# A norm factor by one matmul and a wide power on GpSimd, a last product in column halves, and more fill work before a recurrence's last level

## The chip, the cores and the metric

The kernel runs on one core of a Trainium2 chip. The core has five engines that run side by side and wait for each other through semaphores: TensorE (PE in the profile, with its weight loads as PEld), VectorE (DVE), ScalarE (ACT), GpSimd (POOL) and SyncE (SP, which here only issues DMAs). Matrix products land in PSUM, which DVE and ACT read; everything else lies in SBUF. The metric is device time in microseconds (us) of one execution, lower is better; a time before or after is the median of several executions.

## The reference

One layer of a streaming encoder on 512 tokens of width 1024, batch 1, all in float32. Cut to what matters here:

```python
def rmsnorm(x, g):
    y = x * lax.rsqrt(jnp.mean(x * x, axis=-1, keepdims=True) + EPS)
    return y * g

hn = rmsnorm(h, norm_mix_g[l])
proj = hn @ w_in[l]
fox_out = fox_attention(...)          # 8 heads of 64, causal
rec = hgrn2_chunkwise(...)            # 4 heads, state 128x128, gated recurrence
h = h + jnp.concatenate([fox_out, rec], axis=-1) @ w_out[l]
h = h + memory_cross_attention(rmsnorm(h, norm_x_g[l]), mem_n, w_xq[l], w_xkv[l], w_xo[l])
u = rmsnorm(h, norm_ff_g[l]) @ w1[l]
h = h + jnp.square(jax.nn.relu(u)) @ w2[l]
return rmsnorm(h, final_norm_g)
```

Three places bear on the change: the mean square in the norm ahead of the MLP (`rmsnorm(h, norm_ff_g)`), the MLP's second product (`@ w2`) with the last norm behind it, and the gated recurrence (`hgrn2_chunkwise`).

## The kernel before

Nearly every product is done three times in a reduced float format (hi*hi, lo*hi, hi*lo of operands that ACT and DVE split into a high and a low part), so a product of a 128-wide block of 1024 inputs is 24 matmuls of 128x512. The order on PE is written out by hand; a scheduler sets the order on the other engines from its own estimates.

**The recurrence** (loop over `mlev`, levels m = 1 to 64). At each level ACT builds two `mix` tiles for each of two pairs of heads (L682, L683), PE multiplies them (`lv`, L689), and DVE and POOL update the factors. While these run, PE takes pieces of other projections from a queue `fill`: `fill.run(us)` issues queued matmuls for about so many microseconds, here `2 * F2` = 5.4 behind each level. Ahead of the last level (`li == 6`), `gate_rows` transposes a small tile on PE (`pFr`, L661). The queue holds the projection `gg` there, of which ACT evicts each finished token tile (L588).

**The norm ahead of the MLP.** The residual is held transposed (channels on partitions, the 512 tokens along the free axis). `ssq2` [128x512] sums the squares over the eight channel blocks on POOL (L1038, L1039). `mean_sq` (L1048) sums it over the partitions by four fp32 matmuls with a column of ones, whose result has tokens on partitions ([128x4], `pm`); DVE divides by D, POOL adds EPS (L360, tile `r2e`) and raises it to -1/2 (L363, a `tensor_tensor` with `op=pow` and a tile `mhalf` of -0.5). Four more fp32 matmuls (L1405) spread the four columns over all partitions with the tokens along the free axis again, and DVE copies that to `rbc2` [128x512] (in the profile `rbc`, the tile it shares).

**The MLP.** Hidden blocks are made in eight groups of 512 channels, each four tiles `u` in PSUM (24 matmuls each, L234 to L236). The tiles lie in the pool `mm`, which has three buffers. `square` empties one: DVE multiplies relu(u) by `rbc2` (L1269, tile `ur`), ACT squares it (L1272). So no `u` is emptied before `rbc2` is there, and the fourth `u` tile needs the first one's buffer. In the code `mean_sq` stands between the first and the second `u` tile, the spreading matmuls between the second and the third.

**The second product** is done by a scheme of seven products on quarters (`PRODUCTS`, with `PLAN` for the PSUM bank and where each goes); weight combinations are made by DMAs that add, issued from POOL (L1207). In the last call of `mlp_down` the last product "4" lands in bank `U` behind "1", "6" and "7", for token tile 2 first and tile 3 second; the bank is added to `acc` by DVE (L1299), and `finish` does the last norm of that tile: DVE sum of squares (L1365), POOL power -1/2 (L1367, [128x1]), then ACT (L1369) and DVE (L1371) each scale one half of the columns and two DMAs store them.

Of the kernel before, what the change touches and what calls it, by code (L numbers as in the profile page):

```python
# [12 lines left out]
AF = mybir.ActivationFunctionType  # L13
ALU = mybir.AluOpType
# [19 lines left out]
P1, P2, P3, P4, PW = 20, 20, 20, 10, -20  # L34
MT, NF, V0, LAG = 3, 2, 1, 3
F1, F2, F3, F4, B1 = 1.6, 2.7, 1.5, 1.0, 2.0
A1, A2 = 1.4, 0.8
X1, X2, X3, X4 = 1.5, 2.0, 1.5, 2.0
NEG = -3.0e38
# [3 lines left out]
def emit(  # L43
# [78 lines left out]
    def tr(name, shape=(S,)):  # L122
        return trp.tile([P] + list(shape), F32, tag="tr", name=name)
# [233 lines left out]
    def rstd_of(ms, n, name, r=None):  # L357

        e = sm(n, name + "e")
        gp.tensor_scalar(e, ms, 1.0, EPS, op0=ALU.mult, op1=ALU.add)  # L360
        if r is None:
            r = sm(n, name)
        gp.tensor_tensor(r, e, mhalf[:, 0:n], op=ALU.pow)  # L363
        return r
# [304 lines left out]
    for li, m in enumerate(mlev):  # L669
        if li == 3:  # L670
            fill.until("ff")
            gates()
        if li == 5:
            gate_sums()
        if li == 6:
            gate_rows()
        lvs = []
        for hp in range(2):
            M_ = Mv[hp]
            mix = t2(f"mix{hp}{m}", F32, (NT, P))  # L680
            mv_ = halves(mix.rearrange("p c t -> p (c t)"), m)
            ac.activation(mv_[:, :, 0, :], halves(kt_(2 * hp), m)[:, :, 0, :], AF.Copy)  # L682
            ac.activation(mv_[:, :, 1, :], halves(qt_(2 * hp + 1), m)[:, :, 1, :], AF.Copy)  # L683
            w = 64 if m == 64 else 32
            ps = sc(f"lv{hp}{m}", (NT, 2, w))
            for c in range(NT):
                for o in range(0, P, 2 * w):
                    rhs = bass.AP(M_.tensor, M_.offset + c * P + o + m, [list(M_.ap[0]), [S - m, 2], [2 * m, w // m], [1, m]])
                    te.matmul(ps[o : o + 2 * w, c].rearrange("p u (b m) -> p u b m", m=m), mix[:, c, o : o + 2 * w], rhs, start=True, stop=True)  # L689
            lvs.append(ps)  # L690
        for hp, ps in enumerate(lvs):
            F_ = Fg[hp]
            if m < 64:
                for j in range(2):
                    ve.copy_predicated(
                        Ac[hp][:, 4 * j : 4 * j + 4].rearrange("p c (b two m) -> p c b two m", two=2, m=m)[:, :, :, 1 - j, :],
                        mku[:, j, li, :].rearrange("p (b m) -> p b m", m=m).unsqueeze(1).to_broadcast([P, NT, w // m, m]),
                        ps[:, :, j, :].rearrange("p c (b m) -> p c b m", m=m),
                    )
            else:  # L700
                A_ = s4([8, P], f"A{hp}")
                Ag.append(A_)
                lo_, hi_ = slice(0, 64), slice(64, P)
                gp.memset(A_[hi_, 0:4, lo_], 0.0)
                gp.memset(A_[lo_, 4:8, hi_], 0.0)
                for r in (lo_, hi_):
                    ac.activation(A_[r, :, r], Ac[hp][r], AF.Copy)
                ve.tensor_copy(A_[lo_, 0:4, hi_], ps[lo_, :, 0, :])
                ve.tensor_copy(A_[hi_, 4:8, lo_], ps[hi_, :, 1, :])
            for j in range(2):  # L710
                h = 2 * hp + j
                qv, kv, fv = halves(qt_(h), m), halves(kt_(h), m), halves(F_[:, j, :], m)
                bshape = [P, S // (2 * m), m]
                ve.tensor_tensor(qv[:, :, 1, :], qv[:, :, 1, :], fv[:, :, 0, 0:1].to_broadcast(bshape), ALU.mult)
                (ve, gp)[j].tensor_tensor(kv[:, :, 0, :], kv[:, :, 0, :], fv[:, :, 1, 0:1].to_broadcast(bshape), op=ALU.mult)
            fv = halves(F_.rearrange("p h t -> p (h t)"), m)
            gp.tensor_tensor(fv[:, :, 0, 0:1], fv[:, :, 0, 0:1], fv[:, :, 1, 0:1], op=ALU.mult)
        fill.run(2 * F2)
    fq, fk = {}, {}

    def fox_proj(p):
# [323 lines left out]
    def mean_sq(ssq, name):  # L1045
        pm = tr(name, (NT,))
        for tb in range(NT):
            te.matmul(pm[:, tb : tb + 1], ssq[:, tb * P : (tb + 1) * P], ones, start=True, stop=True)  # L1048
        ms = sm(NT, name + "m")
        ve.tensor_scalar(ms, pm, 1.0 / D, None, op0=ALU.mult)  # L1050
        return ms
# [262 lines left out]
    def mlp_down(gs):  # L1314

        end = gs[-1] == NG - 1
        banks = {}
        for n, name in enumerate(PRODUCTS):
            bank, first_, goes = PLAN[name]

            both = [(g, t) for g in gs for t in range(2)]
            for g, t in both if name != PRODUCTS[-1] else sorted(both, key=lambda gt: gt[1]):
                whi, wlo = unit("d", g, name)
                hb = hbs[g, name]
                if first_ and g == gs[0]:
                    banks[bank, t] = {"U": sc, "Y": tr, "V": mm}[bank](f"{bank}{g}{t}")
                ps = banks[bank, t]
                ts_ = slice(t * P, (t + 1) * P)
                for k in range(2):
                    hi, lo = hb[:, 0, k, ts_], hb[:, 1, k, ts_]  # L1330
                    begin = first_ and g == gs[0] and k == 0
                    te.matmul(ps, hi, whi[:, k, :], start=begin, stop=False, skip_group_check=True)  # L1332
                    te.matmul(ps, hi, wlo[:, k, :], start=False, stop=False, skip_group_check=True)  # L1333
                    te.matmul(ps, lo, whi[:, k, :], start=False, stop=k == 1, skip_group_check=True)  # L1334
                if end and (g, t) == (gs[0], 1) and 1 <= n < len(PRODUCTS) - 1:
                    hidden_part(NG - 1, PRODUCTS[n + 1])
                for rows, half, sign in goes if g == gs[-1] else ():
                    add_to(ps, rows, half, t, sign)
                    if end and (name, rows) in FINAL:
                        finish(2 * rows + t, half)  # L1340
            if not end:
                hidden_part(gs[0] + 1, name)
            elif n == 0:
                hidden_part(NG - 1, PRODUCTS[1])
# [5 lines left out]
    def finish(tb, half):  # L1350

        a = acc[tb]
        cs = slice(half * S, (half + 1) * S)
        if tb not in fin:
            e = sm(1, f"fe{tb}")
            ac.activation(t2(f"fj{tb}"), a[:, cs], AF.Square, scale=1.0 / 32.0, accum_out=e)
            gp.tensor_scalar(e, e, 1.0, EPS, op0=ALU.mult, op1=ALU.add)
            ag = t2(f"fa{tb}")
            gp.tensor_tensor(ag, a[:, cs], gfin[half], op=ALU.mult)
            fin[tb] = (e, cs, ag)  # L1360
            return
        e, cs0, ag = fin[tb]
        o = s4([D], f"fo{tb}")
        v = sm(1, f"fv{tb}")
        ve.tensor_tensor_reduce(out=o[:, cs], in0=a[:, cs], in1=a[:, cs], scale=1.0 / D, scalar=e, op0=ALU.mult, op1=ALU.add, accum_out=v)  # L1365
        r = sm(1, f"fr{tb}")
        gp.tensor_tensor(r, v, mhalf[:, 0:1], op=ALU.pow)  # L1367
        rows = slice(tb * P, (tb + 1) * P)
        ac.activation(o[:, cs0], ag, AF.Identity, scale=r)  # L1369
        ac.dma_start(out[rows, cs0], o[:, cs0])  # L1370
        ve.scalar_tensor_tensor(o[:, cs], a[:, cs], r, gfin[half], op0=ALU.mult, op1=ALU.mult)  # L1371
        nc.sync.dma_start(out[rows, cs], o[:, cs])

    def mlp_up_group(g):
        for j in range(2):
            if g < 2:
                wt = next_panel()
                if (g, j) == (0, 0):
                    down_raws(0)
                elif (g, j) == (1, 1):  # L1380
                    for _ in range(2):
                        unit_q.popleft()[1]()
            else:
                wt = tuple(list(x) for x in zip(*(unit("u", g, j, n) for n in range(2))))
                if (g, j) == (NG - 1, 0):
                    load_raws(g, RAWS[0:3])
            yield from mlp_up(g, j, wt)
# [9 lines left out]
    rbc2 = rbc  # L1397
    ups = mlp_up_group(0)
    up0 = next(ups)
    ms2 = mean_sq(ssq2, "pm2")  # L1400
    r2 = rstd_of(ms2, NT, "r2")
    up1 = next(ups)
    pb = tr("rbc2")
    for tb in range(NT):
        te.matmul(pb[:, tb * P : (tb + 1) * P], r2[:, tb : tb + 1].to_broadcast([P, P]), ident, start=True, stop=True)  # L1405
    ve.tensor_copy(rbc2, pb)
    square(*up0)
    square(*up1)
    for up in ups:
# [42 lines left out]
```

## Time and profile before

| what | value |
|---|---|
| median of 3 executions | 778.06 us (776.39 to 778.52) |
| the profiled execution | 778.45 us |
| its span, first to last instruction | 776.7 us |
| mean granted TensorE clock | 0.996 |
| instructions | 11208 |
| DVE, ACT, POOL busy | 525.6, 367.0, 193.9 us |
| DMA moved | 103.03 MB, mean 133 GB/s |

The time outside the span is 778.45 - 776.7 = 1.75 us. In the profile's rows a group has its line, engine, operation, output and inputs, shape and count, then busy time and mean duration, then the idle time of that engine just before and who ended it. A row of the timeline has start, duration, engine, line, operation and tiles, in microseconds from the span's start.

### The profile page before, as it was taken

What the parts mean: (1) busy time and instruction counts of PE and PEld (TensorE: products, weight loads), DVE (VectorE), ACT (ScalarE), POOL (GpSimd) and SP (SyncE); (2) the same over time, 40 slices, a digit from 0 to 9 for tenths busy, and PEclk for the clock granted to TensorE, in tenths of its full rate; (3) what the DMA queues carried; (4) which work ended last, traced back from release to release, by engine and by line L of the source; (5) the groups of instructions that cost most, each with busy time, mean ns of one, the idle gap of its engine ahead of it and who ended that gap; (6) DMA issues with size and microseconds to landing.
All of it is one profiled execution on the core that took longest, in us unless ns stands there. A gap on an engine that the chain in (4) does not pass through costs nothing.

```text
span 776.7 us, 11208 instructions
## 1 busy us (share of the span) xinstructions
PE 763.2 (98%) x4212; PEld 644.8 (83%) x4212; DVE 525.6 (68%) x846; ACT 367.0 (47%) x616; POOL 193.9 (25%) x262
## 2 busy tenths in 40 slices
PE   7999999999999999999999999999999999999995
PEld 5889988988979988888888888888888888888884
DVE  3746864687577656645538646959686768777795
ACT  4664555675565532344434344535353435352552
POOL 7106532424343015410006520100101010101123
PEclk9999999999999999999999999999999999999998
DMA  6642421142443442312212596575848475758602
GB/s 203 215 127 77 143 83 55 55 130 71 161 136 131 135 156 89 108 57 81 81 54 82 180 281 136 154 172 163 189 136 207 131 181 160 190 136 229 123 1 108
DMA packets 79831, 103.03 MB, mean 133 GB/s; under 512 B 4593, under 2 KB 58394, under 8 KB 79778
## 3 DMA queue, kind: packets, MB, share of 16 engines
q1 hardware_dynamic: 70226, 76.61, 31.3%
q0 software_dynamic: 8960, 24.67, 14.9%
q10 hardware_dynamic: 592, 1.05, 0.4%
q8 instruction: 33, 0.54, 0.3%
q14 instruction: 20, 0.16, 0.1%
HBM read 89.71 MB, written 4.21 MB: 121 GB/s over the span
## 4 chain that ended last, share of the span: by engine, by line
PE 97%; DMA 1%; DVE 1%; issue 0%; POOL 0%; SPq 0%; POOLq 0%; ACT 0%; DVEq 0%; ACTq 0%
PE u L235 7%; PE u L234 7%; PE u L236 7%; PE U L1333 4%; PE U L1334 4%; PE U L1332 3%; PE xq L234 2%; PE xw L234 2%; PE xw L236 2%; PE xq L236 2%; PE xq L235 2%; PE xw L235 2%; PE wo L234 2%; PE wo L236 2%; PE wo L235 2%; PE Y L1333 2%
## 5 line engine op out<-in xcount | busy, mean ns | idle before, releaser
L173 DVE TENSOR_TENSOR wld<-wq,whd 128x1024 fp32r<-128x1024 f32 x56 | 68.7, 1227 | 25.0 <-ACT whd L171 24.8
L234 PE MATMUL u<-x_hi,whu 128*128 128x512 f32 x192 | 74.7, 389 | 0.0
L235 PE MATMUL u<-x_lo,whu 128*128 128x512 f32 x192 | 74.7, 389 | 0.0
L236 PE MATMUL u<-x_hi,wlu 128*128 128x512 f32 x192 | 74.7, 389 | 0.0
L171 ACT ACTIVATE whd<-wq 128x1024 fp32r<-128x1024 f32 x56 | 58.4, 1053 | 30.4 <-PE u L235 21.5
L171 ACT ACTIVATE whu<-wru 128x1024 fp32r<-128x1024 f32 x24 | 25.3, 1053 | 62.0 <-DMA wru<-in_w_dram 62.0
L1207 POOL DMA_DIRECT2D wq<-in_w_dram x16 | 19.5, 1216 | 132.9 <-DMA wq<-in_w_dram 118.7
L173 DVE TENSOR_TENSOR wlu<-wru,whu 128x1024 fp32r<-128x1024 f32 x24 | 29.3, 1221 | 32.7 <-ACT whu L171 32.7
L1332 PE MATMUL U<-whd,hb 128*128 128x512 f32 x128 | 49.8, 389 | 0.0
L1333 PE MATMUL U<-wld,hb 128*128 128x512 f32 x128 | 49.8, 389 | 0.0
L1334 PE MATMUL U<-whd,hb 128*128 128x512 f32 x128 | 49.8, 389 | 0.0
L1207 POOL DMA_DIRECT2D wq<-wq x16 | 14.0, 878 | 122.5 <-DVE wld L173 96.0
L234 PEld LDWEIGHTS u<-x_hi,whu 128*128 128x128 f32 x192 | 36.0, 188 | 7.5
L235 PEld LDWEIGHTS u<-x_lo,whu 128*128 128x128 f32 x192 | 36.0, 188 | 7.5
L236 PEld LDWEIGHTS u<-x_hi,wlu 128*128 128x128 f32 x192 | 36.0, 188 | 7.4
L902 POOL TENSOR_SCALAR bi<-nF,Ft 128x128 f32<-128x128 f32 (+3 forms) x32 | 22.4, 700 | 42.5 <-PE pt L929 20.3
L1272 ACT ACTIVATE sq<-ur 128x512 f32<-128x512 f32 x32 | 20.0, 626 | 26.3 <-DVE ur L1269 26.3
L1269 DVE SCALAR_TENSOR_TENSOR ur<-u,rbc 128x512 f32<-128x512 f32 x32 | 21.9, 687 | 12.4 <-PE u L236 12.4
L919 ACT ACTIVATE bi<-bi,mx 128x128 f32<-128x128 f32 (+3 forms) x32 | 17.9, 560 | 23.3 <-DVE mx L917 23.1
L1332 PEld LDWEIGHTS U<-whd,hb 128*128 128x128 f32 x128 | 24.0, 188 | 5.0
L1334 PEld LDWEIGHTS U<-whd,hb 128*128 128x128 f32 x128 | 24.0, 188 | 5.0
L1333 PEld LDWEIGHTS U<-wld,hb 128*128 128x128 f32 x128 | 24.0, 188 | 5.0
(934 smaller groups left out, 2355.8 us busy)
## 6 DMA issues: line engine op xcount, KB each, us to landing
wq<-in_w_dram SPq DMA_DIRECT2D x40, 512.0 KB, 3.4
wru<-in_w_dram SPq DMA_DIRECT2D x24, 512.0 KB, 3.8
wq<-in_w_dram POOLq DMA_DIRECT2D x16, 512.0 KB, 8.4
wq<-wq POOLq DMA_DIRECT2D x16, 512.0 KB, 4.6
xTd<-xT POOLq DMA_DIRECT2D x4, 512.0 KB, 3.1
nF<-Fd POOLq DMA_DIRECT2D x8, 256.0 KB, 4.3
hT<-xTd POOLq DMA_DIRECT2D x4, 512.0 KB, 4.1
xt<-in_x_dram SPq DMA_DIRECT2D x3, 512.0 KB
```

Of the source, the lines that this page charges most:

```text
L171: ac.activation(hi, raw, AF.Copy)
L173: ve.tensor_tensor(lo, raw, f(hi), ALU.subtract)
L234: te.matmul(ps, wh, hi, start=n_ == 0, stop=False)
L235: te.matmul(ps, wh, lo, start=False, stop=False)
L236: te.matmul(ps, wl, hi, start=False, stop=n_ == KC - 1)
L902: gp.tensor_scalar(bi[:, 0:n], fF[h][:, 0:n], -1.0, Ft[:, tb, h : h + 1], op0=ALU.mult, op1=ALU.add)
L1207: gp.dma_start(raw.rearrange("p (k n) -> p k n", k=2), src, accum_op=ALU.add)
L1269: ve.scalar_tensor_tensor(u, ps, 0.0, rbc2, op0=ALU.max, op1=ALU.mult)
L1272: ac.activation(sqs[g, j][:, i, :], u, AF.Square)
L1332: te.matmul(ps, hi, whi[:, k, :], start=begin, stop=False, skip_group_check=True)
L1333: te.matmul(ps, hi, wlo[:, k, :], start=False, stop=False, skip_group_check=True)
L1334: te.matmul(ps, lo, whi[:, k, :], start=False, stop=k == 1, skip_group_check=True)
```

## The change

It has three parts. (1) `mean_sq`, the power on [128x4] and the spreading matmuls are replaced: one fp32 matmul with a 128x128 block of ones gives the sum of squares of each token on all partitions at once ([128x512]); DVE scales it and adds EPS; POOL raises the whole [128x512] tile to -1/2. (2) In the last call of `mlp_down`, what bank `U` of token tile 3 holds is added to `acc` ahead of product "4"; that product is done for tile 3 in two halves of 256 columns, each in a bank of its own (`Z`), and `finish_half` sums the squares by halves. (3) `fill.run` behind level `li == 5` gets 1.2 us more, so more queued matmuls stand ahead of the last level.

```diff
+FL = 1.2
...
-        fill.run(2 * F2)
+
+        fill.run(2 * F2 + (FL if li == 5 else 0.0))
...
+            last = end and name == PRODUCTS[-1]
             both = [(g, t) for g in gs for t in range(2)]
-            for g, t in both if name != PRODUCTS[-1] else sorted(both, key=lambda gt: gt[1]):
+            if last:
+                add_to(banks["U", 1], 1, 0, 1, 1)
+                both = [(g, 0) for g in gs]
+            for g, t in both:
...
+            if last:
+                for q in range(2):
+                    qs = slice(q * HS, (q + 1) * HS)
+                    ps = mm(f"Z{q}")[:, 0:HS]
+                    steps = [(g, k, a, b) for g in gs for k in range(2) for a, b in ((0, 0), (0, 1), (1, 0))]
+                    for i, (g, k, a, b) in enumerate(steps):
+                        hb, w = hbs[g, name], unit("d", g, name)
+                        te.matmul(ps, hb[:, a, k, P : 2 * P], w[b][:, k, qs], start=i == 0, stop=i == len(steps) - 1)
+                    piece = acc[3][:, qs]
+                    ve.tensor_tensor(piece, ps, piece, ALU.add)
+                    finish_half(q, qs)
...
+    def finish_half(q, qs):
+
+        e, cs0, ag = fin[3]
+        a = acc[3]
+        if q == 0:
+            fin["o"] = s4([D], "fo3")
+            fin["v"] = [sm(1, f"fv3{i}") for i in range(2)]
+        o, v = fin["o"], fin["v"]
+        ve.tensor_tensor_reduce(out=o[:, qs], in0=a[:, qs], in1=a[:, qs], scale=1.0 / D, scalar=(e, v[0])[q], op0=ALU.mult, op1=ALU.add, accum_out=v[q])
+        if q == 0:
+            return
+        r = sm(1, "fr3")
+        gp.tensor_tensor(r, v[1], mhalf[:, 0:1], op=ALU.pow)
+        rows, cs = slice(3 * P, NT * P), slice(0, S)
+        ac.activation(o[:, cs0], ag, AF.Identity, scale=r)
+        ac.dma_start(out[rows, cs0], o[:, cs0])
+        ve.scalar_tensor_tensor(o[:, cs], a[:, cs], r, gfin[0], op0=ALU.mult, op1=ALU.mult)
+        nc.sync.dma_start(out[rows, cs], o[:, cs])
...
-    ms2 = mean_sq(ssq2, "pm2")
-    r2 = rstd_of(ms2, NT, "r2")
+
+    pb = tr("rbc2")
+    te.matmul(pb, ones.to_broadcast([P, P]), ssq2, start=True, stop=True)
+    ve.tensor_scalar(rbc2, pb, 1.0 / D, EPS, op0=ALU.mult, op1=ALU.add)
+    gp.tensor_tensor(rbc2, rbc2, mhalf[:, 0:1].to_broadcast([P, S]), op=ALU.pow)
     up1 = next(ups)
-    pb = tr("rbc2")
-    for tb in range(NT):
-        te.matmul(pb[:, tb * P : (tb + 1) * P], r2[:, tb : tb + 1].to_broadcast([P, P]), ident, start=True, stop=True)
-    ve.tensor_copy(rbc2, pb)
     square(*up0)
```

How the rows of the engines move, at three places (a row is line, operation, output<-inputs, shape of the output, and what the row waits for; "Pool" is GpSimd, "Activation" ScalarE).

GpSimd at the start of the MLP, before; the DMAs are the adding ones of the first weight group:

```order
L1039 TENSOR_TENSOR ssq_4182<-ssq_4182,xwsq_4614 128x512 [waits Pool_49]
L1207 DMA wq_4630<-in_w_dram 128x2x512 [waits DMAHW1_49,PE_49]
L360 TENSOR_SCALAR r2e<-pm2m 128x4 [waits DVE_49]
L1207 DMA wq_4630<-in_w_dram 128x2x512 [waits DMAHW2_49]
L363 TENSOR_TENSOR r_4694<-r2e,mhalf 128x4 [waits Pool_49]
L1207 DMA wq_4631<-in_w_dram 128x2x512 [waits DMAHW0_49,PE_49,Activation_49]
```

The same place on GpSimd with the change:

```order
L1041 TENSOR_TENSOR ssq_4182<-ssq_4182,xwsq_4614 128x512 [waits Pool_49]
L1209 DMA wq_4630<-in_w_dram 128x2x512 [waits DMAHW1_49,PE_49]
L1209 DMA wq_4630<-in_w_dram 128x2x512 [waits DMAHW2_49]
L1440 TENSOR_TENSOR rbc<-rbc,mhalf 128x512 [waits DVE_49]
L1209 DMA wq_4631<-in_w_dram 128x2x512 [waits DMAHW0_49,PE_49,Activation_49]
```

The small power of four columns has become one of 512 columns, behind the same two DMAs and ahead of the same third. VectorE at this place with the change (`wl` are the low parts of weights, `ht` the last transposed residual):

```order
L1138 COPY acc_4347<-ht_4676 128x128 [waits Activation_49]
L1439 TENSOR_SCALAR rbc<-rbc_4685 128x512 [waits PE_49]
L1138 COPY acc_4349<-ht_4676 128x128 [waits Activation_49]
L1271 SCALAR_TENSOR_TENSOR ur_4714<-u_4651,rbc 128x512 [waits Pool_49]
L174 TENSOR_TENSOR wl36a<-wr36a,wh36a 128x1024 [waits DMAHW7_49,PE_49,Activation_49]
L1271 SCALAR_TENSOR_TENSOR ur_4718<-u_4689,rbc 128x512 [waits PE_49]
L174 TENSOR_TENSOR wl36b<-wr36b,wh36b 128x1024 [waits DMAHW5_49,Activation_49]
```

The first `ur` now waits for GpSimd, and the splits of the weights of the second group stand behind it; before, that split `wl36a` came ahead of the copy to `rbc`, and the first `ur` behind both.

ScalarE ahead of the recurrence's last level, before (`wh9a` is the high part of a later weight, `gg` the projection's tiles evicted, `mix` built for the level):

```order
L171 ACTIVATE wh9a<-wr9a 128x1024 [waits DMAHW3_49,PE_49,Activation_49]
L588 ACT_TABLE_LOAD
L588 ACTIVATE gg_1000<-gg_1002,r_383 128x512 [waits PE_49]
L588 ACTIVATE gg_1000<-gg_1003,r_383 128x512 [waits PE_49]
L682 ACTIVATE mix_1255<-sta_406 128x4x64
L683 ACTIVATE mix_1255<-sta_406 128x4x64
L682 ACTIVATE mix_1263<-sta_409 128x4x64
```

And with the change:

```order
L172 ACTIVATE wh9a<-wr9a 128x1024 [waits DMAHW3_49,PE_49,Activation_49]
L589 ACT_TABLE_LOAD
L589 ACTIVATE gg_1000<-gg_1002,r_383 128x512 [waits PE_49]
L589 ACTIVATE gg_1000<-gg_1003,r_383 128x512 [waits PE_49]
L589 ACTIVATE gg_1001<-gg_1004,r_383 128x512 [waits PE_49]
L683 ACTIVATE mix_1262<-sta_406 128x4x64
L684 ACTIVATE mix_1262<-sta_406 128x4x64
```

The third eviction of `gg` has moved ahead of the `mix` tiles. VectorE at the end of the program, before (ISA is the sum of squares L1365, a row without inputs reads its accumulator):

```order
L1299 TENSOR_TENSOR acc_4348<-U_6846,acc_4348 128x512 [waits PE_49]
L1365 ISA fo_7121,fv_7122<-acc_4348,fe_7038 128x512 [waits DVE_49]
L1365 ISA fv_7122 128x1
L1371 SCALAR_TENSOR_TENSOR fo_7121<-acc_4348,fr_7124,gfin_4626 128x512 [waits Pool_49]
L1299 TENSOR_TENSOR acc_4349<-U_6853,acc_4349 128x512 [waits PE_49]
L1365 ISA fo_7143,fv_7144<-acc_4349,fe_7051 128x512 [waits DVE_49]
```

And with the change:

```order
L1382 ISA fo_7109,fv_7110<-acc_4348,fe_7025 128x512 [waits DVE_49]
L1382 ISA fv_7110 128x1
L1356 TENSOR_TENSOR acc_4349<-Z_7118,acc_4349 128x256 [waits PE_49]
L1388 SCALAR_TENSOR_TENSOR fo_7109<-acc_4348,fr_7112,gfin_4626 128x512 [waits Pool_49]
L1399 ISA fo_7132,fv_7133<-acc_4349,fe_7038 128x256 [waits DVE_49]
L1399 ISA fv_7133 128x1
L1356 TENSOR_TENSOR acc_4349<-Z_7136,acc_4349 128x256 [waits PE_49]
L1399 ISA fo_7132,fv_7134<-acc_4349,fv_7133 128x256 [waits DVE_49]
```

The addition of the first half stands ahead of tile 2's scaling (L1388), which waits for GpSimd; the rest of tile 3 stays behind it.

## The prediction

> **What bounds the kernel now.** I read the page first: its span, the busy time of each engine and the chain that ended last.
>
> ```profile
> span 776.7 us, 11208 instructions
> PE 763.2 (98%) x4212; PEld 644.8 (83%) x4212; DVE 525.6 (68%) x846; ACT 367.0 (47%) x616; POOL 193.9 (25%) x262
> PE 97%; DMA 1%; DVE 1%; issue 0%; POOL 0%; SPq 0%; POOLq 0%; ACT 0%; DVEq 0%; ACTq 0%
> ```
>
> TensorE is busy for 98% and is 97% of the chain, so there are 13.5 us in all in which it does nothing. The view of waits, for TensorE alone, says how little of that any engine causes inside the program:
>
> ```profile
> PE xn L423 <- DMA xt<-in_x_dram: 2.8, 1, 2.8
> PE lv L689 <- issue: 0.6, 1, 0.6
> ```
>
> 2.8 us are the first load and 0.6 us the last level of the recurrence; the tail behind the last matmul has most of the rest. So the kernel gets faster only by fewer TensorE microseconds, by that 0.6 us, or by a shorter tail, and gets slower one for one with each new TensorE wait. My sum is made against the profiled execution's 778.45 us, which lies 0.4 us above the median 778.06 us; differences under about 0.3% (2.3 us) a measurement of this kernel can't tell from none.
>
> **The norm factor, and the term that decides.** The timeline of TensorE at the start of the MLP:
>
> ```profile
> 445.24 0.95 PE L1048 MATMUL pm<-ones,ssq 128*128 128x1 f32 x8
> 446.05 0.48 PE L234 MATMUL u<-x_hi,wh34a 128*128 128x512 f32 x1
> 451.60 1.05 PE L1405 MATMUL rbc<-ident,r 128*128 128x128 f32 x8
> 452.41 0.48 PE L234 MATMUL u<-x_hi,wh35a 128*128 128x512 f32 x1
> 457.97 0.39 PE L234 MATMUL u<-x_hi,wh35a 128*128 128x512 f32 x1
> ```
>
> Each of the two groups of small fp32 products holds TensorE for 0.81 us until the next `u` matmul starts (446.05 - 445.24 and 452.41 - 451.60). The second group goes: -0.8. The first becomes one fp32 product of 512 columns, which no row shows. In L1405 eight passes of 128 columns take 0.81, and two passes of 512 columns stream as many columns: 0.8, so no difference. As fast as reduced-format matmuls (24 of them from 452.41 to 457.97, 0.23 each) it would be 0.5; at 1.2 it would cost 0.4.
>
> At 457.97 the fourth `u` tile starts. It needs the buffer of the first, which L1269 empties, and that needs `rbc2`. With the change GpSimd's power on 512 columns stands before it. GpSimd's place for it, the emptying, and a split of weights on VectorE:
>
> ```profile
> 448.29 1.51 POOL L363 TENSOR_TENSOR r<-r2e,mhalf 128x4 f32<-128x4 f32 x1
> L1269 DVE SCALAR_TENSOR_TENSOR ur<-u,rbc 128x512 f32<-128x512 f32 x32 | 21.9, 687 | 12.4 <-PE u L236 12.4
> L173 DVE TENSOR_TENSOR wld<-wq,whd 128x1024 fp32r<-128x1024 f32 x56 | 68.7, 1227 | 25.0 <-ACT whd L171 24.8
> ```
>
> The power of four columns, behind the same two DMA issues, ends at 449.80 (448.29 + 1.51). What would 512 columns take? The trace has powers of one and of four columns; I asked for the rows of their lines, and for the plain multiply-add ahead of one of them:
>
> ```profile
> L363 POOL TENSOR_TENSOR m0r<-m0re,mhalf x1: 572/572/572, 118.8 to 118.8; 128x1 f32<-128x1 f32 x1
> L1367 POOL TENSOR_TENSOR fr<-fv,mhalf x4: 543/548/566, 763.1 to 770.8; 128x1 f32<-128x1 f32 x4
> L363 POOL TENSOR_TENSOR hr<-hr2e,mhalf x1: 1007/1007/1007, 142.5 to 142.5; 128x4 f32<-128x4 f32 x1
> L363 POOL TENSOR_TENSOR r<-r0e,mhalf x1: 1085/1085/1085, 27.5 to 27.5; 128x4 f32<-128x4 f32 x1
> L360 POOL TENSOR_SCALAR hr2e<-hs x1: 192/192/192, 142.3 to 142.3; 128x4 f32<-128x4 f32 x1
> L1035 POOL TENSOR_TENSOR ssq<-hT 128x512 f32<-128x512 f32 x2 | 2.1, 1037 | 24.7 <-DVE hT L1031 24.7
> ```
>
> One column takes about 0.555 us, four about 1.02: three more columns cost 0.465, so **0.155 us a column**. A multiply-add of four columns takes 0.19, so the 0.8 above it is the power's own work. Four one-column powers in a row (L1367) agree within 5%, so this is no first-use cost. On this line 508 more columns cost 78.7 us. The bounds: the lowest slope of these rows is (1.007 - 0.572)/3 = 0.145, the highest (1.085 - 0.543)/3 = 0.181; all of a four-column power above 0.19 shared by four is 0.208; from below stands L1035, a plain multiply of the full shape, in 1.04. I take 0.155, since those rows are the same operation, though 512 columns lie far outside them.
>
> The Trainium skill, "GPSIMD Engine Reference", section 3.1 on elementwise cycle accounting, gives about 2.6 cycles per element for a two-input elementwise operation and 4497 ns for 2048 columns; by it 512 columns would be an estimated 1.1 us, and the sum below would end at 777.3. L1035 agrees with that page for a multiply; the power's rows do not.
>
> Then: the power ends at 449.80 + 78.7 = 528.5. DVE's first `ur`, queued right behind that wait, takes 0.69; with 0.1 for two hand-overs the fourth `u` tile starts at 529.3 in place of 457.97: **+71.3**. The 0.8 saved ahead of it is lost in the wait. Behind the waiting `ur` on VectorE stand the splits of the next weights (1.2 us each) and two more `ur`; together about 4 us, beside the fourth tile's 5.5, so no second wait follows. GpSimd's next adding DMAs are issued right as TensorE resumes, as early against it as before.
>
> After such a pause TensorE starts slow. The rows of the start show it, and the window after the last matmul shows the clock falling in idle time:
>
> ```profile
> 8.23 1.11 PE L423 MATMUL xn<-ident,xt 128*128 128x128 f32 x4 [2.79 <-DMA xt<-in_x_dram]
> 9.57 0.63 PE L235 MATMUL gf<-hn_lo,wh0a 128*128 128x512 f32 x1
> 10.00 0.63 PE L236 MATMUL gf<-hn_hi,wl0a 128*128 128x512 f32 x1
> 13.41 0.42 PE L236 MATMUL gf<-hn_hi,wl0a 128*128 128x512 f32 x1
> 768.00:776.70 8.70, 0.21 (x1) 0.00 (x0) 2.86 (x5) 1.44 (x2) 1.09 (x2) 0.68 0.41 156
> ```
>
> From 8.23 to about 13.4 a 512-column matmul comes every 0.43 instead of 0.23; in some 4.5 us ten matmuls lose 0.2 each: **+2.0** (bounds 0 and 2.5).
>
> **More fill ahead of the last level.** TensorE and ScalarE there:
>
> ```profile
> 112.47 0.60 PE L661 MATMUL pFr<-ident,Ft 128*8 128x128 f32 x4
> 113.67 2.02 PE L689 MATMUL lv<-mov,mix 128*128 128x128 f32 x16 [0.60 <-issue]
> 111.69 1.26 ACT L588 ACTIVATE gg<-gg,r 128x512 f32<-128x512 f32 x2
> 113.16 0.41 ACT L683 ACTIVATE mix<-sta 128x256 f32<-128x256 f32 x1
> ```
>
> `lv` starts as the first pair's `mix` is done (113.57). Six matmuls (six times 0.23, 1.4 us) now stand before `pFr`, so TensorE arrives 1.4 later. But ScalarE now evicts a third `gg` tile ahead of `mix`: its last matmul starts at 112.9, so the eviction runs from about 113.4 for 0.6, and `mix` follows by 114.7. `lv` starts at about 114.8, 1.1 later for 1.4 of work: **-0.25**, between 0 and -0.7. The six matmuls are taken from later filling, where other queued work takes their place.
>
> **The tail.** The end of the program, engines mixed:
>
> ```profile
> 767.82 0.39 PE L1334 MATMUL U<-whd,hb 128*128 128x512 f32 x1
> 768.04 0.54 POOL L1367 TENSOR_TENSOR fr<-fv,mhalf 128x1 f32<-128x1 f32 x1 [2.26 <-DVE fv L1365]
> 768.62 0.75 DVE L1371 SCALAR_TENSOR_TENSOR fo<-acc,fr,gfin 128x512 f32<-128x512 f32 x1 [0.66 <-POOL fr L1367]
> 769.29 0.68 DVE L1299 TENSOR_TENSOR acc<-U,acc 128x512 f32<-128x512 f32 x1
> 770.01 0.75 DVE L1365 CUSTOM_DVE_ANT_0 fo<-acc,fe 128x512 f32<-128x512 f32 x1
> 770.85 0.54 POOL L1367 TENSOR_TENSOR fr<-fv,mhalf 128x1 f32<-128x1 f32 x1 [2.26 <-DVE fv L1365]
> ...
> L631 DVE TENSOR_TENSOR Ac<-dg,id 128x256 f32<-128x256 f32 x4 | 1.7, 418 | 0.6 <-PE dg L628 0.6
> L917 DVE CUSTOM_DVE_ANT_0 bi<-ps,bi 128x256 f32<-128x256 f32 x8 | 3.4, 423 | 2.1 <-PE ps L912 2.0
> ...
> 339.13 0.28 PE L1088 MATMUL xs<-kT,xqh 128*128 128x256 f32 x1
> 340.56 0.40 PE L234 MATMUL xq<-x_hi,wh27b 128*128 128x512 f32 x1
> ```
>
> The last matmul is done at 768.2, yet its addition starts at 769.29: VectorE first scales token tile 2. So the tail is VectorE's, not TensorE's. The halves cost TensorE little: twelve 256-column matmuls take 1.43 (339.13 to 340.56), 24 take 2.87, against 12 times 0.23; 0.1 later, with 1 us to spare. On VectorE the first half's addition fits into the 0.66 idle ahead of 768.62. From 769.29 then come sum of squares, addition, sum of squares of 256 columns, 0.42 each, with hand-overs 1.5, where addition and sum now take 1.56 (769.29 to 770.85): **-0.1**, between -0.4 and +0.3. The addition of bank `U` ahead of product "4" is 0.7 of VectorE time in a place that waits for TensorE's later products, and costs nothing.
>
> **Sum.** 71.3 - 0.25 + 2.0 - 0.1 = +73.0 us: **851.4 us**, 9.4% slower. With slopes 0.145 and 0.181 it is 846 and 865, with 0.208 it is 877.
>
> **Rivals.** *The power runs at nearly the plain rate on long rows* (the other side: not slower). The work of one and four columns would then be start-up and a loop that overlaps only when long. It must end by about 456.4, 0.8 ahead of the fourth tile's new start, so in 7.6 us or 15 ns a column; then only savings are left: -0.8 - 0.25 - 0.1, **777.3 us**, which is no measurable change. For it speaks L1035 with 2 ns a column, against it that the step from one to four columns is ten times 15 ns. *A loop in between*, 20 to 100 ns a column: the power takes 10 to 51 us and the kernel 780 to 823, middle 803. Nothing in the rows points to a particular value. *The fill doesn't fill its gap*, since `mix` moves along: +0.25 against the sum, inside the range. *The tail gets longer*, if the sums of squares of 256 columns cost as much as of 512: +0.3, too little to decide a sign.
>
> **How the numbers follow.** The rows of the same operation carry the forecast: 0.62. The loop in between 0.14, the plain rate 0.24. The forecast's own range is 845 to 866. With only 0.76 on stalls and part of them above 866, the range reaches down to the plain rate: 776 to 866. Slower by over 0.3%: 0.62 + 0.14 = 0.76. Within: 0.21 of the plain rate; faster 0.03, if its terms all fall at their good ends (-1.1, -0.7 and -0.4, together -2.2) and the measurement adds to that.
>
> **What would show it.** In the profile after: one POOL row of the power on 128x512, near 80 us; a TensorE wait of near 70 us on the fourth `u` tile, released over L1269; 0.43 between the first matmuls behind it; a wait of about 0.5 left ahead of the last level; and a tail from the end of tile 2's scaling of the same length as now. A power under 8 us proves the main term wrong, and then the sign is decided by tenths.

## The result, and the profile after

| | before | after |
|---|---|---|
| median | 777.61 us (776.39 to 778.52, 4 runs) | 851.52 us (851.34 to 851.9, 4 runs) |
| the profiled execution, its span | 778.45, 776.7 | 851.9, 849.9 |
| mean granted TensorE clock | 0.996 | 0.95 |

The ratio is 1.0953, with a 95% interval of 1.0941 to 1.0966: the changed kernel is 9.5% slower. The page of the profile after, its parts on busy times, slices (busy tenths of 40 equal slices, and the granted clock), chain and groups:

```profile
span 849.9 us, 11199 instructions
...
PE 763.9 (90%) x4210; PEld 644.2 (76%) x4210; DVE 525.7 (62%) x849; ACT 366.8 (43%) x616; POOL 275.5 (32%) x261
...
PE   8999999999999999999994000999999999999996
PEclk9999999999999999999997555999999999999998
...
PE 87%; POOL 10%; DMA 1%; DVE 1%; issue 0%; SPq 0%; POOLq 0%; ACT 0%; DVEq 0%; ACTq 0%
...
L1440 POOL TENSOR_TENSOR rbc<-rbc,mhalf 128x512 f32<-128x512 f32 x1 | 82.6, 82616 | 0.0
L1271 DVE SCALAR_TENSOR_TENSOR ur<-u,rbc 128x512 f32<-128x512 f32 x32 | 22.0, 688 | 95.9 <-POOL rbc L1440 83.1
```

TensorE does as much as before (763.9 us of work against 763.2), but three and a half of the forty slices are empty, and the granted clock falls to 0.5 in them. GpSimd, which was 0% of the chain, is 10% of it, with one instruction. The view of waits, for TensorE alone (what waits, for whom, total, times, longest):

```profile
PE u L235 <- DVE ur L1271: 73.9, 1, 73.9
PE xn L424 <- DMA xt<-in_x_dram: 1.6, 2, 1.1
```

Nearly the whole loss is one wait that was not there before: the fourth `u` tile for the buffer that the first `ur` empties. The only other new wait in this view is 0.4 us of `gf` at the start of the program. The timeline shows what stands behind that release, first on GpSimd and VectorE:

```profile
443.79 2.55 POOL L1209 DMA_DIRECT2D wq<-in_w_dram  x2 [2.62 <-PE ht L1132]
444.35 0.69 DVE L1439 TENSOR_SCALAR rbc<-rbc 128x512 f32<-128x512 f32 x1 [0.26 <-PE rbc L1438]
445.71 82.62 POOL L1440 TENSOR_TENSOR rbc<-rbc,mhalf 128x512 f32<-128x512 f32 x1
528.36 0.69 DVE L1271 SCALAR_TENSOR_TENSOR ur<-u,rbc 128x512 f32<-128x512 f32 x1 [83.11 <-POOL rbc L1440]
```

The record of the power begins at 445.71, while the two DMA issues ahead of it on GpSimd last until 446.34 (443.79 + 2.55); so the power proper is taken to run from there to 528.33, 82.0 us. (The four-column power of the kernel before has the same overlap: its record begins at 448.29, the DMA issue ahead of it ends at 448.73, and from there to its end are 1.07 us, like the other four-column powers.) Then TensorE, around the norm, behind the pause, and ahead of the recurrence's last level:

```profile
112.16 0.60 PE L662 MATMUL pFr<-ident,Ft 128*8 128x128 f32 x4
113.08 2.02 PE L690 MATMUL lv<-mov,mix 128*128 128x128 f32 x16 [0.32 <-issue]
...
443.29 1.02 PE L1438 MATMUL rbc<-ssq,ones 128*128 128x512 f32 x2
443.75 0.79 PE L235 MATMUL u<-x_hi,wh34a 128*128 128x512 f32 x1
444.38 0.39 PE L236 MATMUL u<-x_lo,wh34a 128*128 128x512 f32 x1
...
529.10 0.79 PE L235 MATMUL u<-x_hi,wh35a 128*128 128x512 f32 x1 [73.89 <-DVE ur L1271]
529.69 0.63 PE L236 MATMUL u<-x_lo,wh35a 128*128 128x512 f32 x1
...
533.53 0.42 PE L236 MATMUL u<-x_lo,wh35a 128*128 128x512 f32 x1
```

From these rows the whole difference of the two profiled spans, 849.9 - 776.7 = 73.2, can be split at two marks, the start of the norm's product and the start of the fourth `u` tile:

| stretch | before | after | difference |
|---|---|---|---|
| start to the norm's product (L1048, L1438) | 445.24 | 443.29 | -1.95 |
| norm's product to the fourth `u` tile | 12.73 | 85.81 | +73.08 |
| fourth `u` tile to the end | 318.73 | 320.80 | +2.07 |

Of the 1.95 in the first line, 0.28 is the wait ahead of `lv` (0.60, now 0.32). The other 1.7 are there already at `pFr`, which starts 0.31 earlier with six more matmuls (1.4 us) ahead of it; 1.2 of that is the first load, on which TensorE waited 2.8 us in one execution and 1.6 in the other; the new wait of `gf` takes 0.4 back, and the rest is likely the slow pace of the first matmuls, which lasts to 13.41 in the kernel before and to about 11.4 here. The first wait is 1.3 in one and 2.6 in another of the kernels below that have no pause, so this line of the table is put down to the execution and not to the change.

The end of the program on VectorE, the scaling of token tile 2 and the scaling of tile 3:

```profile
842.00 0.75 DVE L1388 SCALAR_TENSOR_TENSOR fo<-acc,fr,gfin 128x512 f32<-128x512 f32 x1 [0.32 <-POOL fr L1384]
...
844.68 0.75 DVE L1407 SCALAR_TENSOR_TENSOR fo<-acc,fr,gfin 128x512 f32<-128x512 f32 x1 [0.66 <-POOL fr L1403]
```

From one scaling to the other it is 2.68 us (842.00 to 844.68). In the kernel before the scaling of tile 2 stands at 768.62, and that of tile 3, from the same view, here:

```profile
771.43 0.75 DVE L1371 SCALAR_TENSOR_TENSOR fo<-acc,fr,gfin 128x512 f32<-128x512 f32 x1 [0.66 <-POOL fr L1367]
```

That was 2.81, so the halves gain 0.13 between these two executions.

### The profile page after: what moved, and what is told of

The parts are those of the page before. It is cut to its first block, busy times and chain, and to the rows that moved or that the text cites. A ratio compares the mean times of both kernels' runs of the same rounds, so it can differ in the third digit from the quotient of the medians.

```text
span 849.9 us, 11199 instructions
## 1 busy us (share of the span) xinstructions
PE 763.9 (90%) x4210; PEld 644.2 (76%) x4210; DVE 525.7 (62%) x849; ACT 366.8 (43%) x616; POOL 275.5 (32%) x261
## 4 chain that ended last, share of the span: by engine, by line
PE 87%; POOL 10%; DMA 1%; DVE 1%; issue 0%; SPq 0%; POOLq 0%; ACT 0%; DVEq 0%; ACTq 0%
POOL rbc L1440 10%; PE u L235 7%; PE u L236 6%; PE u L237 6%; PE U L1338 3%; PE U L1339 3%; PE U L1340 3%; PE xq L235 2%; PE xw L235 2%; PE xw L237 2%; PE xq L237 2%; PE xq L236 2%; PE xw L236 2%; PE wo L235 2%; PE wo L236 2%; PE wo L237 2%
## 5 line engine op out<-in xcount | busy, mean ns | idle before, releaser
L1440 POOL TENSOR_TENSOR rbc<-rbc,mhalf 128x512 f32<-128x512 f32 x1 | 82.6, 82616 | 0.0
L1271 DVE SCALAR_TENSOR_TENSOR ur<-u,rbc 128x512 f32<-128x512 f32 x32 | 22.0, 688 | 95.9 <-POOL rbc L1440 83.1
L235 PE MATMUL u<-x_hi,wh35a 128*128 128x512 f32 x8 | 4.2, 528 | 73.9 <-DVE ur L1271 73.9
L235 PEld LDWEIGHTS u<-x_hi,wh35a 128*128 128x128 f32 x8 | 2.0, 253 | 74.7 <-DVE ur L1271 74.3
L1340 PE MATMUL U<-whd,hb 128*128 128x512 f32 x124 | 48.3, 389 | 0.0
L1338 PE MATMUL U<-whd,hb 128*128 128x512 f32 x124 | 48.2, 389 | 0.0
```

The costliest lines, as they stand in the source:

```text
L235: te.matmul(ps, wh, hi, start=n_ == 0, stop=False)
L1271: ve.scalar_tensor_tensor(u, ps, 0.0, rbc2, op0=ALU.max, op1=ALU.mult)
L1440: gp.tensor_tensor(rbc2, rbc2, mhalf[:, 0:1].to_broadcast([P, S]), op=ALU.pow)
```

## The experiments

Two theories could explain a slowdown of this size. **Theory A**, the prediction's: the power's time on GpSimd grows by a fixed price for each column, and the kernel pays it one for one. **Theory B**: something else than the count of columns makes this one instruction slow (the broadcast exponent, the full tile, its place beside the DMAs), or parts 2 and 3 have a share. Eight kernels ran. All but one did all of the kernel's work; what is left out or added is said with each.

**Parts 2 and 3 alone** (`parts_2_3`): part 1 undone.

```diff
-    te.matmul(pb, ones.to_broadcast([P, P]), ssq2, start=True, stop=True)
-    ve.tensor_scalar(rbc2, pb, 1.0 / D, EPS, op0=ALU.mult, op1=ALU.add)
-    gp.tensor_tensor(rbc2, rbc2, mhalf[:, 0:1].to_broadcast([P, S]), op=ALU.pow)
+    ms2 = mean_sq(ssq2, "pm2")
+    r2 = rstd_of(ms2, NT, "r2")
```

(and the four spreading matmuls with their copy, as before.)

> The changed kernel with its first part undone (mean_sq, the power on 128x4 and the four spreading products are back). My theory: the whole slowdown is the wide power, so this is within 0.5 us of before: the fill gives 0.3 (TensorE wait ahead of the last level 0.3 instead of 0.6), the tail 0.1. Rival, some of the 74 us comes from the other two parts (a product in a bank of its own, halves, the moved fill): this is slower than before by more than 2 us.

Measured: 776.36 us (776.04 to 777.23) beside 776.5 of the kernel before on the same chip, ratio 0.9995, interval 0.9986 to 1.0004. The wait ahead of `lv` is 0.3 here too. So fill and halves together make no difference that can be measured, and the slowdown is none of theirs.

**Part 1 alone** (`part_1`): the four lines of part 1 in the kernel before, nothing else; its lines are numbered otherwise (L1269 is the same statement as L1271).

> The kernel before with the first part alone (one matmul with ones, wide power on GpSimd). My theory: 851.9 us, 0.4 above the changed kernel, with a power row of 82.6 us and a TensorE wait of 74 us behind it. Rival (another part carries some of it): well under 850.

Measured, in one run: 852.29. Its view of waits has the wait in full:

```profile
PE u L234 <- DVE ur L1269: 74.1, 1, 74.1
```

With the kernel above this settles which part it is.

**Half of the power** (`half_pow`): only the first 256 columns are raised to -1/2; the norm factor of the other 256 tokens stays unraised.

```diff
-    gp.tensor_tensor(rbc2, rbc2, mhalf[:, 0:1].to_broadcast([P, S]), op=ALU.pow)
+    gp.tensor_tensor(rbc2[:, 0:256], rbc2[:, 0:256], mhalf[:, 0:1].to_broadcast([P, 256]), op=ALU.pow)
```

> The changed kernel with the power on the first 256 of 512 columns only; the other half of the norm factor is left unraised. My theory, 0.16 us a column: the power row falls from 82.6 to about 41.7 us and the time by 40.9, to 810.6. Rival (a price of the wide instruction as such, from a different loop or from its neighbours on the memory ports): not in proportion, above 825 or below 795.

Measured: 811.41. The group of the power in its page, and its wait:

```profile
L1440 POOL TENSOR_TENSOR rbc<-rbc,mhalf 128x256 f32<-128x256 f32 x1 | 41.9, 41867 | 0.0
```

```profile
PE u L235 <- DVE ur L1271: 33.2, 1, 33.2
```

256 columns fewer take 40.7 us less on GpSimd (82.6 - 41.9), 0.159 a column, and TensorE waits 40.7 less (73.9 - 33.2). The time fell by 40.1 (851.52 - 811.41). The price is by the column and is paid one for one, as theory A has it; a fixed cost of the place or of the form would have stayed.

**Powers of eight widths** (`pow_widths`): the kernel before, with eight extra powers of 1 to 128 columns on a tile of constants, whose results nobody reads. Their exponent is broadcast as in the change.

```diff
+    pwi, pwo = t3("pwi"), t3("pwo")
+    gp.memset(pwi, 2.0)
+    for n in (1, 2, 4, 8, 16, 32, 64, 128):
+        gp.tensor_tensor(pwo[:, 0:n], pwi[:, 0:n], mhalf[:, 0:1].to_broadcast([P, n]), op=ALU.pow)
```

> The kernel before with eight extra powers on GpSimd, of 1, 2, 4, 8, 16, 32, 64 and 128 columns of a constant, with the exponent broadcast as in the change, in a stretch where GpSimd is idle for 54 us; their results are not used. My theory, a line through the small powers: 0.40 + 0.155 n us, so 0.56, 0.71, 1.0, 1.6, 2.9, 5.4, 10.3, 20.2, and a time within noise of before. Rivals: the broadcast exponent makes it slow (then the row of 4 is well above the 1.02 of the rows with a full operand), or a slower loop sets in at some width (then a step between two of the rows).

The view of groups by shape, GpSimd (busy, mean ns of one, idle time before it), without the rows of other instructions between them:

```profile
L1083 POOL TENSOR_TENSOR pwo<-pwi,mhalf 128x128 f32<-128x128 f32 x1 | 20.7, 20726 | 0.1
L1083 POOL TENSOR_TENSOR pwo<-pwi,mhalf 128x64 f32<-128x64 f32 x1 | 10.5, 10522 | 0.0
L1083 POOL TENSOR_TENSOR pwo<-pwi,mhalf 128x32 f32<-128x32 f32 x1 | 5.4, 5438 | 0.0
L1083 POOL TENSOR_TENSOR pwo<-pwi,mhalf 128x16 f32<-128x16 f32 x1 | 2.9, 2895 | 0.1
L1083 POOL TENSOR_TENSOR pwo<-pwi,mhalf 128x4 f32<-128x4 f32 x1 | 2.0, 2002 | 0.1
L1083 POOL TENSOR_TENSOR pwo<-pwi,mhalf 128x8 f32<-128x8 f32 x1 | 1.6, 1634 | 0.1
L1083 POOL TENSOR_TENSOR pwo<-pwi,mhalf 128x2 f32<-128x2 f32 x1 | 0.8, 798 | 0.0
L1083 POOL TENSOR_TENSOR pwo<-pwi,mhalf 128x1 f32<-128x1 f32 x1 | 0.6, 581 | 4.1 <-ACT bi L919 4.1
```

From 64 to 128 columns it is (20726 - 10522) / 64 = 0.159 us a column, from 16 to 32 also 0.159, from 2 to 8 only 0.139. One straight line, 0.4 + 0.159 for each column, runs from 16 columns through 256 (41.1; measured 41.2, without the overlap with the DMA issue) to 512 (81.8, measured 82.0). From 16 columns on nothing steps, and nothing overlaps on longer rows. The slope is the same at another place of the program, so the place beside the MLP's DMAs isn't the cause.

One row does not fit: four columns took 2.00, 1 us above the line. The expectation named a four-column row well above 1.02 as the sign that the broadcast exponent is slow. But the rows of two and of eight columns have the same broadcast exponent, and by the slope between them four columns would take 1.08, where an exponent of full width took 1.007 to 1.085 in the kernel before. So the broadcast has no price for each column that these rows show; what held up this one row stays open (GpSimd issues no DMA in that time). A wide power with an exponent of full width was not run. With that said, theory B has nothing left that could make up 82 us.

The time of this kernel missed what was expected: 813.99. The scheduler put the extra powers beside the attention, at 226.9 to 274 us, where the tiles `bi` that VectorE waits for come from GpSimd. The view of waits, TensorE:

```profile
PE pt L929 <- DVE bi L921: 26.6, 1, 26.6
PE pv L945 <- DVE pts L935: 6.2, 1, 6.2
```

These two waits are 32.8 of the 37.4 us lost; the rest is likely the clock, whose granted mean is 0.67 from 244 to 252 and 0.60 from 276 to 281, behind each of them. So 45 us of idle GpSimd time can't be had for nothing wherever it is taken: GpSimd is busy for a quarter of the span in all, but in that stretch others wait for it.

**The power on ScalarE** (`ln_exp`): the same value as exp(-1/2 ln x), by two activations of the whole tile; all else as changed.

```diff
-    gp.tensor_tensor(rbc2, rbc2, mhalf[:, 0:1].to_broadcast([P, S]), op=ALU.pow)
+    ac.activation(rbc2, rbc2, AF.Ln)
+    ac.activation(rbc2, rbc2, AF.Exp, scale=-0.5)
```

> The changed kernel with the power moved to ScalarE, as exp(-0.5 ln x) on 128x512. My theory: two table loads of 1.3 and two activations of 0.6 us, 3.8 in all, end about 449, 5 us ahead of the fourth u tile's start, so nothing waits, and the change's small savings are left: 0.8 of TensorE time, 0.3 of fill, 0.1 of tail, 776.4 us against 777.6 before. Rival (that the single fp32 product of 512 columns, or the order of VectorE with the first ur ahead of the weights, costs something of its own that the long wait hid): 778 or more.

Measured: 775.42 us (774.24 to 776.95, 11 runs) beside 776.5 of before, ratio 0.9982, interval 0.9973 to 0.9991. ScalarE's timeline at the place:

```profile
444.69 1.28 ACT L1440 ACT_TABLE_LOAD   x1
445.99 0.63 ACT L1440 ACTIVATE rbc<-rbc 128x512 f32<-128x512 f32 x1
446.64 1.28 ACT L1441 ACT_TABLE_LOAD   x1
447.93 0.63 ACT L1441 ACTIVATE rbc<-rbc 128x512 f32<-128x512 f32 x1
```

The factor is there at 448.56, 3.9 us after the first table load began, in place of 82; the first `ur` starts at 448.60 and the wait on the fourth `u` tile is gone from the view. This is the best of the versions, 0.12% faster than `parts_2_3` (776.36) and about 0.2% faster than before, which is little, though the interval leaves out 1. What part 1 can bring is the second group of small products that it saves, 0.8 by the prediction's rows. The 0.9 between the medians of these two kernels agrees with it, though their ranges overlap, and the trace shows it: the norm's product starts at 443.56 and the fourth `u` tile at 455.33, 11.77 apart where the kernel before has 12.73. The idea of one product was good; the engine of the power was not.

**TensorE kept busy in the pause** (`warm_stall`, then `warm_stall_2`): 2.1 us of the loss lie behind the pause. To see if they come from the slower clock or from what stands behind the wait, extra matmuls of 512 columns fill the pause, into a bank that nobody reads; 310 of them, and 323 in the second kernel.

```diff
     up1 = next(ups)
+    up2 = next(ups)
+    busy = pvt("busy")
+    for _ in range(310):
+        te.matmul(busy, x2_hi[:, 0, 0:P], x2_hi[:, 0, :], start=True, stop=True)
     square(*up0)
     square(*up1)
+    square(*up2)
```

> The changed kernel with 310 further matmuls of 128x512 on TensorE between the third and the fourth u tile, into a bank of their own that nothing reads: 310 times 0.2275 = 70.5 us, inside the wait of 73.9. My theory: the wait is set by GpSimd alone and stays otherwise, 3.4 us of it are left idle, but the matmuls behind it start at 0.23 instead of 0.43 us each, so the time falls by 2.1 us to 849.4. Rival (the slow first matmuls come from weights or from VectorE behind the wait, not from the pause): no change, 851.5.

Measured: 852.25 us (851.22 to 852.44), no gain over 851.52 (ratio to before 1.0954 to 1.099, where the changed kernel has 1.0941 to 1.0966). The timeline of TensorE where the extra matmuls end:

```profile
528.79 0.50 PE L235 MATMUL u<-x_hi,wh35a 128*128 128x512 f32 x1 [3.47 <-DVE ur L1271]
529.12 0.39 PE L236 MATMUL u<-x_lo,wh35a 128*128 128x512 f32 x1
529.36 0.45 PE L237 MATMUL u<-x_hi,wl35a 128*128 128x512 f32 x1
529.60 0.63 PE L235 MATMUL u<-x_hi,wh35a 128*128 128x512 f32 x1
530.03 0.63 PE L236 MATMUL u<-x_lo,wh35a 128*128 128x512 f32 x1
...
532.59 0.58 PE L236 MATMUL u<-x_lo,wh35a 128*128 128x512 f32 x1
```

The extra matmuls ended 3.47 us too early, and that much idle time was enough to bring the slow pace back: three matmuls at 0.33 and 0.24, then 0.43 until 532.59. From the restart to the end of the span are 320.7 us (849.5 - 528.79), about as many as in the changed kernel (320.8). The expectation missed because the experiment still had a pause, not because the clock was shown not to matter. The Trainium skill, "TensorE: Matmul & The Clock Gate", Part 1, "What's actually happening", says that an idle window of about 3.4 us halves the clock, and that the window runs on its own beat. The pause of 3.47 agrees with the first. The granted clock fell 3.3 us after the last matmul in the changed kernel (455.2 to 458.5), and here 4.3 us after it (525.3 to 529.6), which would fit the second, but no run here tests it. So 13 more were added, and the changed kernel ran again on the same chip (`after_again`):

> The changed kernel with 323 extra matmuls of 512 columns in the pause, into a bank that nobody reads: 13 more than the run before, so that about 0.5 us of TensorE's wait stays instead of 3.5. If a pause of 3.5 us is enough to bring the slow clock back and one of 0.5 is not, the first matmuls of the fourth u tile stand 0.23 apart throughout and the time is 2.1 below that of the changed kernel on the same chip (about 849.4 where that is 851.5). Rival: the loss behind the pause is not the clock's, and the time is that of the changed kernel.

> The changed kernel as it is, for a comparison on the same chip: 851.5, with ten matmuls 0.43 apart behind the pause.

The first matmuls behind the pause in `warm_stall_2`, from its timeline:

```profile
530.81 0.50 PE L235 MATMUL u<-x_hi,wh35a 128*128 128x512 f32 x1 [0.92 <-DVE ur L1271]
531.14 0.39 PE L236 MATMUL u<-x_lo,wh35a 128*128 128x512 f32 x1
531.38 0.39 PE L237 MATMUL u<-x_hi,wl35a 128*128 128x512 f32 x1
531.61 0.40 PE L235 MATMUL u<-x_hi,wh35a 128*128 128x512 f32 x1
```

And in `after_again`:

```profile
528.14 0.80 PE L235 MATMUL u<-x_hi,wh35a 128*128 128x512 f32 x1 [74.21 <-DVE ur L1271]
528.73 0.63 PE L236 MATMUL u<-x_lo,wh35a 128*128 128x512 f32 x1
...
530.86 0.50 PE L235 MATMUL u<-x_hi,wh35a 128*128 128x512 f32 x1
```

The view of windows has the granted clock (the first number behind the busy times of the five engines) from 528 to 536, in the changed kernel, in `warm_stall` and in `warm_stall_2`:

```profile
528.00:536.00 8.00, 6.90 (x21) 5.50 (x22) 5.77 (x7) 4.43 (x6) 0.50 (x2) 0.65 0.57 189
528.00:536.00 8.00, 7.21 (x25) 5.77 (x26) 5.98 (x7) 4.53 (x6) 0.28 (x2) 0.79 0.61 204
528.00:536.00 8.00, 7.08 (x32) 5.53 (x31) 4.86 (x6) 3.67 (x6) 2.03 (x1) 1.00 0.36 122
```

With 0.92 us of pause left the matmuls stand 0.23 apart at a clock of 1.00; after 74.21 they stand 0.43 apart, and in such a stretch the granted clock is 0.50 (528.1 to 530.8 in `after_again`, 529.1 to 533.5 in the changed kernel). From the restart to the end of the span `warm_stall_2` takes 849.5 - 530.81 = 318.7, just what the kernel before takes (318.73); `after_again`, of span 848.3, takes 320.2, and the changed kernel 320.8. So the term behind the pause is the clock, worth 1.5 and 2.1 us in these two executions: six matmuls were slow in `after_again`, not the ten that were expected. The medians, 850.98 (849.82 to 851.23) and 852.21 (850.2 to 853.68), differ by 1.2 in the expected direction where 2.1 was expected, and the two ranges overlap. The two profiled spans even go the other way (849.5 and 848.3), since the norm's product starts 2.75 us later in `warm_stall_2` (444.75 and 442.00), ahead of the pause. The stretch behind the restart decides it, not the times.

## Why the prediction was right, step by step

**The main term.** The prediction took the power on a line through its rows of one and four columns, 0.155 us a column. The mechanism was right and the size a little small: 0.159 on longer rows, and 82.0 us where the prediction's line gives 79.7. The beginning of the line is uneven (from one to two columns 0.217, from two to eight 0.139 in `pow_widths`), so a slope taken there was low by 3%, which 508 columns turned into 2.3 us. That it was no further off is in part luck: the rows of two and eight columns alone would have given 72 us. Against these 2.3 us, the power starts sooner behind the norm's product than was assumed: 3.05 us (443.29 to 446.34) where the old four-column power started some 3.5 behind its own (445.24 to 449.80, less its 1.02). GpSimd's small addition and one hand-over ahead of it are gone, which the prediction left out. Together the stretch grew by 73.08 where +71.3 was foretold: 1.8 too little. (One bound was added up wrongly: with the slope of 0.208 the prediction's own terms come to 878, not 877.)

**The slow clock.** +2.0 foretold, +2.16 by the pace: ten matmuls from 529.10 to 533.53 took 4.43 where 2.27 would do. The start of the kernel before gave the right size. That the slow pace there has the same cause is likely but not shown: the changed kernel's own start has the pace of 0.43 at a granted clock of 0.50 (8.2 to 9.5), as behind the pause, but for the start of the kernel before the profile gives 1.00 (8.2 to 13.4).

**The ones product.** Taken as no difference, 0.8 for 0.8. From its start to the second `u` matmul behind it are 1.09 us (443.29 to 444.38). It holds TensorE for 0.46 before the next matmul starts, which then takes longer. In the kernel before the same stretch is 1.13 (445.24 to 446.37), so no difference was right. Its price doesn't matter in the changed kernel, since anything saved there is lost in the wait.

**The fill.** -0.25 foretold, -0.28 measured. The prediction's signs speak of a wait of about 0.5 left, but its own sum leaves 0.35 (0.60 - 0.25), and 0.32 was left. The reason given fits, that the third `gg` eviction moves ahead of `mix` and takes back about half of the 0.60 that could be gained; its rows:

```profile
111.68 0.69 ACT L589 ACTIVATE gg<-gg,r 128x512 f32<-128x512 f32 x1 [0.39 <-PE gg L265]
112.27 0.41 ACT L683 ACTIVATE mix<-sta 128x256 f32<-128x256 f32 x1
```

The pair's `mix` starts right behind that eviction. That the six matmuls come off later filling and not off the end, `parts_2_3` bears out only as far as its time goes: no difference.

**The tail.** -0.1 foretold, -0.13 measured.

**The sum.** The terms as measured are 73.08 - 0.28 + 2.07 (clock and tail) = +74.9, where the prediction had +73.0; the profiled spans differ by 73.2, since the start took 1.7 less. That the predicted 851.4 still lies within 0.2 us of the median is partly chance: the sum was made against an execution 0.8 us above the median of before (778.45 and 777.61), and the wait for the first load moves spans by more than a microsecond, as the 1.7 us in the profile after show. What was right is the mechanism, its place and 97% of its size (73.0 of 74.9).

**The rivals.** The plain rate is out: the power takes some 80 times the 1.04 us of the multiply of the same shape. The loop in between is out: one straight line runs from 16 to 128 columns in `pow_widths` and on to the 256 and 512 of the other kernels. The rule of the Trainium skill, "GPSIMD Engine Reference", section 3.1, by which the power would have taken an estimated 1.1 us, is not borne out for this operation, only for the multiply. That the fill or the tail would decide a sign was never reached.

## What to carry to other kernels

Before a small operation is made wide, look for rows of that same operation at two sizes: the slope tells more than the row of another operation at the full size, and two short rows foretold 82 us to within 3% here, with some luck: wider rows, where a trace has them, are the safer base. Spreading the mean square first and raising it afterwards multiplied the columns of the power by 128, so a costly function belongs on the compact form, or on an engine whose price for a column is small. An instruction that every emptying of a buffer waits for is hidden only as long as the free buffers last, here about 8 us (82.0 of power, 73.9 of wait).

## What the runs showed of the hardware

GpSimd's power costs 0.159 us for each column of 128 partitions from 16 columns on, where its multiply of 512 columns takes 1.04 us in all. The same value by Ln and Exp on ScalarE took 0.63 us each for 512 columns, with a table load of 1.28 ahead of each. A pause of 3.47 us on TensorE brought the slow pace back at a granted clock of 0.50, though only 0.8 us after the restart, and one of 0.92 didn't; nothing between the two was tried. The length of the slow stretch is not fixed: ten matmuls in the one profiled execution of the changed kernel, six in the other.
